# An NSA / RG-LRU decoder layer on one core: x^T split unscaled, the input norm's weight moved into the projection weights, and the residual rebuilt from the two halves

## The chip, the cores and the metric

The kernel runs on one core of one Trainium2 chip. The metric is the device time of one execution in microseconds (us). Single runs of this kernel lie within about 0.3% of each other, so a difference below that can't be told from none.

## What is computed

One step of a one-layer hybrid decoder on a prompt (1024 tokens) and a sample group (8 sequences of 4 tokens), with the same weights. All 1056 tokens go through the same projection; `TOK` is 1056, `D` is 1024. The part that the change touches is the entry of the layer and its first residual:

```python
def rmsnorm(x, g):
    xf = x.astype(jnp.float32)
    y = xf * lax.rsqrt(jnp.mean(xf * xf, axis=-1, keepdims=True) + EPS) * g.astype(jnp.float32)
    return y.astype(x.dtype)
...
u = rmsnorm(x, lw['norm_mix'])
q, q_rot, kv_rows, win_rows, gates, rg, rx = project(u, lw['w_in'], pos)
...
mixed = jnp.concatenate([rmsnorm(o_attn, lw['g_attn']),
                         rmsnorm(jax.nn.gelu(rg) * h_rnn, lw['g_rnn'])], axis=-1)
x = x + mixed @ lw['w_out']
v = rmsnorm(x, lw['norm_mlp'])
x = x + jnp.square(jax.nn.relu(v @ lw['w_up'])) @ lw['w_down']
```

Between them lie three attention branches (compressed, selected, windowed) and a gated linear recurrence (RG-LRU).

## The kernel before

**Precision.** Each float32 product is made of three TensorE products of a value's rounded half and its remainder: `split` (L126) writes `hi` with ScalarE (ACT, L127) and `lo = src - hi` with VectorE (DVE, L128), and `mm3` (L120) adds hi*hi, hi*lo and lo*hi in PSUM.

**Load.** `fetch_x` (L269) reads nine tiles of x, 128 tokens each (the last 32), into eight buffers. `load_x` (L237) takes them in three groups of up to 384 tokens; for each of 8 blocks of 128 features, TensorE transposes (L257) into a PSUM tile `ps_x`. From it ACT writes `u_hi`, scaled by `norm_mix` (`g_mix`, L261), DVE writes `u_lo` (L262), and one of the two copies it unscaled to `xr` (L265), which goes to DRAM as `xT` in twelve DMAs issued by GpSimd (POOL, L267). The row sums of squares come from ACT (L249); the factor 1/rms per token is applied after the projection, through the tile `R`: `bcast_all` (L1150) builds it from diagonal tiles `dg` (DVE, L1159), a product with ones (`ps_bc`, L1160) and an ACT copy (L1162).

**Projection.** `in_proj` (L305) does 128 columns of `w_in` at a time: `w_tile_` (L293) loads the raw tile `wraw` (one buffer, SP queue) and splits it to `wh`, `wl` (two buffers); 72 products follow, in three token chunks of 352, and DVE evacuates each chunk times `R` (L322, L366). There are 18 such tiles: two for the compressed keys and values, four each for the two RG-LRU branches (`rx`, `rg`), two window tiles (`zw`), two more and four for the queries. `gates` (L753) loads 24 columns in the same way.

**Compression of the cached pages.** `cmp_setup` (L449) loads and splits two weight tiles `cwraw` (one buffer; `lo` on POOL); `cmp_cached` (L571) loads 16 tiles of two pages (`lpg`, three buffers; half by the SP queue after a register load for each, L543 and L553, half by POOL, L557), copies them on POOL and DVE (`lpr`, L592), transposes (`ps_ct`, L599) and projects (`ps_c`).

**RG-LRU.** `rglru` (L355) and `rg_gate` (L415) do convolution (DVE, L384), gates, a scan (L405) and products on POOL (L398, L427, L439).

**Residual.** `rnn_proj` (L1164) reads each block of `xT` back (`xres`, L1189), POOL adds the projected RG-LRU result (L1197), and the sum is stored. The small vectors (`vectors`, L190) arrive through nine DMAs of POOL into `rows`, kept in the pool `xrp`.

**Order.** A scheduler places the instructions on each engine's queue, which then runs strictly in that order; `high_priority` lets weight tiles be placed early.

Of the kernel before, what the change touches and what calls it, by code (L numbers as in the profile page):

```python
# [9 lines left out]
F32 = mybir.dt.float32  # L10
# [3 lines left out]
AF = mybir.ActivationFunctionType  # L14
ALU = mybir.AluOpType
# [3 lines left out]
D = 1024  # L19
# [3 lines left out]
TOK = SEQ + NS * QS  # L23
CH = 352
NCH = 3
KT = 8
# [79 lines left out]
class K:  # L106
# [83 lines left out]
    def vectors(self):  # L190
        nc, a = self.nc, self.a
        rows = self.xrp.tile([56, 128], F32, name="rows")
# [44 lines left out]
    def load_x(self):  # L237
        nc, a = self.nc, self.a
        self.u = [self.up.tile([128, KT, TOK], F32R, name=n) for n in ("u_hi", "u_lo")]
        uh, ul = self.u  # L240
        self.stores = {}
        self.xT = self.dp.tile([KT, 128, TOK], F32, name="xT_dram")
        self.ss = self.cp.tile([128, 9], F32, name="ss")
        nc.vector.memset(self.ss, float(D))
        for grp in range(3):
            tiles = self.xt[grp * 3 : grp * 3 + 3]
            for t, (xt, n) in enumerate(tiles):
                junk = self.xtp.tile([128, D], BF16, tag="xj", name="xj", bufs=1)
                nc.scalar.activation(junk[:n], xt[:n], AF.Square, accum_out=self.ss[:n, grp * 3 + t : grp * 3 + t + 1])  # L249
            wdt = sum(n for _, n in tiles)  # L250
            c0 = grp * 384
            for kb in range(KT):
                pool, tag = ((self.ps_tp, "tp"), (self.ps_mm, "mm"))[kb % 2]
                ps = pool.tile([128, 512], F32, tag=tag, name="ps_x")
                o = 0
                for xt, n in tiles:
                    nc.tensor.transpose(ps[:, o : o + n], xt[:n, kb * 128 : kb * 128 + 128], self.ident[:n, :n])  # L257
                    o += n
                g = self.g_mix[:, kb : kb + 1]
                hi, lo = uh[:, kb, c0 : c0 + wdt], ul[:, kb, c0 : c0 + wdt]  # L260
                nc.scalar.activation(hi, ps[:, :wdt], AF.Copy, scale=g)  # L261
                nc.vector.scalar_tensor_tensor(lo, ps[:, :wdt], g, hi.bitcast(F32), ALU.mult, ALU.subtract)  # L262
                if kb % 2 == 0:
                    xr = self.xrp.tile([128, 2, 384], F32, tag="xr", name="xr", bufs=5)
                (nc.scalar.copy if kb % 4 == 0 else nc.vector.tensor_copy)(xr[:, kb % 2, :wdt], ps[:, :wdt])  # L265
                if kb % 2:
                    self.stores[grp, kb] = nc.gpsimd.dma_start(self.xT[kb - 1 : kb + 1, :, c0 : c0 + wdt].rearrange("k p t -> p k t"), xr[:, :, :wdt])  # L267

    def fetch_x(self):  # L269
# [3 lines left out]
        for t in range(9):  # L273
            n = 128 if t < 8 else 32
            xt = self.xtp.tile([128, D], F32, tag="xt", name="xt", bufs=8)
# [17 lines left out]
    def w_tile_(self, c0, m):  # L293
# [5 lines left out]
        nc.sync.dma_start(raw[:, :, :m], src)  # L299
        wh = self.wp.tile([128, KT, 128], F32R, tag="wh", name="wh", bufs=1)  # L300
        wl = self.wp.tile([128, KT, 128], F32R, tag="wl", name="wl", bufs=1)
        self.split(wh[:, :, :m], wl[:, :, :m], raw[:, :, :m])
        return wh, wl

# [144 lines left out]
    def cmp_setup(self):  # L449
# [11 lines left out]
        for i, kv in enumerate("kv"):  # L461
            raw = self.cwp.tile([128, 8, 2, 64], F32, tag="cwraw", name="cwraw", bufs=1)
# [290 lines left out]
    def gates(self):  # L753
# [5 lines left out]
        nc.sync.dma_start(raw[:, :, :24], self.a["w_in"][0].rearrange("(k p) f -> p k f", p=128)[:, :, c0 : c0 + 24])  # L759
        w = self.wp.tile([128, KT, 128], F32R, tag="wh", name="wh", bufs=1)  # L760
# [403 lines left out]
    def rnn_proj(self):  # L1164
# [11 lines left out]
        for dp in range(4):  # L1176
# [8 lines left out]
            for d2 in range(2):  # L1185
# [3 lines left out]
                nc.sync.dma_start(xt, self.xT[d])  # L1189
# [264 lines left out]
    def run(self):  # L1454
# [11 lines left out]
        with ExitStack() as PA:  # L1466
# [3 lines left out]
            with ExitStack() as s:  # L1470
# [5 lines left out]
                with ExitStack() as s2:  # L1476
                    self.xtp = self.pool(s2, "xtp")
                    self.xrp = self.pool(s2, "xrp")
# [6 lines left out]
                    self.vectors()  # L1485
# [5 lines left out]
                zs = [self.z_tile(512 + i * 128, self.zp, "z", 2) for i in range(2)]  # L1491
                self.cmp_cached()
# [136 lines left out]
```

## Time and profile before

| | |
|---|---|
| three runs | 1571.28, 1572.1, 1576.55 us (median 1572.1) |
| profiled execution | 1577.57 us, span 1575.8 us |
| busy share of the span | PE 95%, DVE 57%, ACT 40%, POOL 30% |
| granted TensorE clock, mean | 0.984 |
| DMA | 107.14 MB, 89.79 read and 19.93 written |

PE is TensorE's products, PEld its weight loads. A name like `L592 DVE COPY lpr<-lpg` gives the line of the kernel, the engine, the operation, and what is written from what. SPq is the DMA queue of the SP engine. In a timeline a number in brackets is the idle time of the engine before the instruction, and what ended it.

### The profile page before, as it was taken

The numbers are of one execution on the slowest core, as the hardware profiler recorded it, in microseconds if no ns is written. First come the engines' busy times: TensorE is split into PE (matmuls) and PEld (weight loads), VectorE is DVE, ScalarE is ACT, GpSimd is POOL, SyncE is SP. The second block draws the span as 40 slices with busy tenths as digits, with TensorE's granted clock in tenths as the row PEclk, the third lists the DMA queues.
The fourth block names the chain that finished last, engine by engine and source line by source line (L and its number), as shares of the span: only waits on it lengthen the run. The fifth ranks groups of instructions, "written<-read, shape, count | busy, mean of one in ns | idle before, by whom it ended". The sixth has DMA issues, their size and how long they took to land.

```text
span 1575.8 us, 24404 instructions
## 1 busy us (share of the span) xinstructions
PE 1501.3 (95%) x9439; PEld 1403.2 (89%) x9439; DVE 893.3 (57%) x1674; ACT 623.5 (40%) x1208; POOL 467.0 (30%) x535
## 2 busy tenths in 40 slices
PE   5889999999998999999998999999999999999997
PEld 3879998899766777768898999999999999999997
DVE  7464688657633888899888343433434333343445
ACT  6254685222234888877444031220303122030322
POOL 6450233342624878766673000000000000000012
PEclk9999999999998999999999999999999999999999
DMA  9431111453640000000512020230202021020102
GB/s 294 133 108 37 41 41 30 159 195 103 195 127 1 1 1 1 1 27 27 164 30 79 14 81 27 82 131 14 81 14 81 27 60 49 15 80 14 41 11 101
DMA packets 103768, 107.14 MB, mean 68 GB/s; under 512 B 16112, under 2 KB 90544, under 8 KB 103524
## 3 DMA queue, kind: packets, MB, share of 16 engines
q1 hardware_dynamic: 96718, 89.51, 18.6%
q0 software_dynamic: 4736, 12.86, 2.6%
q10 hardware_dynamic: 2198, 3.20, 0.6%
q8 instruction: 74, 1.21, 0.3%
q14 instruction: 42, 0.34, 0.1%
HBM read 89.79 MB, written 19.93 MB: 70 GB/s over the span
## 4 chain that ended last, share of the span: by engine, by line
PE 77%; DVE 11%; ACT 4%; issue 3%; POOL 2%; DMA 2%; SPq 1%; DVEq 0%; ACTq 0%; POOLq 0%
PE ps_dn L122 8%; PE ps_dn L123 8%; PE ps_dn L124 8%; PE ps_up L122 7%; PE ps_up L123 7%; PE ps_up L124 7%; PE ps_in L122 3%; PE ps_in L123 3%; PE ps_in L124 3%; PE ps_T L1079 3%; PE ps_so L967 2%; PE ps_O L1089 2%; PE ps_S L1047 2%; PE ps_O L1088 1%; PE ps_S L1048 1%
## 5 line engine op out<-in xcount | busy, mean ns | idle before, releaser
L122 PE MATMUL ps_up<-v_hi,wuh 128*128 128x352 f32 x768 | 248.8, 324 | 0.0
L122 PE MATMUL ps_dn<-hh,wdh 128*128 128x352 f32 x768 | 248.3, 324 | 0.0
L123 PE MATMUL ps_up<-v_lo,wuh 128*128 128x352 f32 x768 | 247.0, 322 | 0.0
L124 PE MATMUL ps_up<-v_hi,wul 128*128 128x352 f32 x768 | 246.8, 321 | 0.0
L123 PE MATMUL ps_dn<-hl,wdh 128*128 128x352 f32 x768 | 245.9, 321 | 0.0
L124 PE MATMUL ps_dn<-hh,wdl 128*128 128x352 f32 x768 | 245.5, 321 | 0.0
L1348 DVE TENSOR_TENSOR x<-x,ps_dn 128x352 f32<-128x352 f32 x192 | 99.3, 521 | 222.2 <-PE ps_dn L124 222.1
L1413 POOL TENSOR_TENSOR facc<-facc,fsq 128x352 f32<-128x352 f32 x18 | 17.0, 944 | 700.0 <-ACT fsq L1411 699.8
L127 ACT CAST wdh<-wd 128x1024 fp32r<-128x1024 f32 x32 | 33.5, 1047 | 341.9 <-PE ps_dn L123 288.7
L123 PEld LDWEIGHTS ps_up<-v_lo,wuh 128*128 128x128 f32 x768 | 144.9, 189 | 0.0
L122 PEld LDWEIGHTS ps_up<-v_hi,wuh 128*128 128x128 f32 x768 | 144.6, 188 | 0.0
L124 PEld LDWEIGHTS ps_up<-v_hi,wul 128*128 128x128 f32 x768 | 144.5, 188 | 0.0
L123 PEld LDWEIGHTS ps_dn<-hl,wdh 128*128 128x128 f32 x768 | 144.2, 188 | 0.0
L122 PEld LDWEIGHTS ps_dn<-hh,wdh 128*128 128x128 f32 x768 | 144.1, 188 | 0.0
L124 PEld LDWEIGHTS ps_dn<-hh,wdl 128*128 128x128 f32 x768 | 143.9, 188 | 0.0
L122 PE MATMUL ps_in<-u_hi,wh 128*128 128x352 f32 x432 | 142.8, 331 | 0.9 <-DVE sp_acc L229 0.9
L124 PE MATMUL ps_in<-u_hi,wl 128*128 128x352 f32 x432 | 141.6, 328 | 0.0
L123 PE MATMUL ps_in<-u_lo,wh 128*128 128x352 f32 x432 | 141.4, 327 | 0.0
L128 DVE TENSOR_TENSOR ptl<-ps_T,pth 128x512 fp32r<-128x512 f32 x132 | 88.0, 683 | 13.7 <-ACT pth L127 12.6
L127 ACT CAST pth<-ps_T 128x512 fp32r<-128x512 f32 (+1 forms) x148 | 83.3, 588 | 18.7 <-PE ps_T L1079 14.8
L122 PEld LDWEIGHTS ps_in<-u_hi,wh 128*128 128x128 f32 x432 | 83.2, 193 | 1.5 <-issue 1.3
L123 PEld LDWEIGHTS ps_in<-u_lo,wh 128*128 128x128 f32 x432 | 83.3, 193 | 0.1
(506 smaller groups left out, 3320.6 us busy)
## 6 DMA issues: line engine op xcount, KB each, us to landing
wu<-in_w_up_dram SPq DMA_DIRECT2D x32, 512.0 KB
wd<-in_w_down_dram SPq DMA_DIRECT2D x32, 512.0 KB
wraw<-in_w_in_dram SPq DMA_DIRECT2D x18, 512.0 KB
lpg<-in_cache_kv_dram SPq DMA_DIRECT2D x64, 128.0 KB
xres<-xT_dram SPq DMA_DIRECT2D x8, 528.0 KB
x_dram<-xres SPq DMA_DIRECT2D x8, 528.0 KB
x<-x_dram SPq DMA_DIRECT2D x3, 1408.0 KB
xt<-in_x_prompt_dram SPq DMA_DIRECT2D x8, 512.0 KB
```

The source lines that it names most:

```text
L122: t.matmul(out, wh, xh, start=first, stop=False)
L123: t.matmul(out, wh, xl, start=False, stop=False)
L124: t.matmul(out, wl, xh, start=False, stop=last)
L127: self.nc.scalar.copy(hi, src)
L128: (eng or self.nc.vector).tensor_tensor(lo, src, hi.bitcast(F32), ALU.subtract)
L967: T.matmul(po[w, :128], l, r, start=n == 0, stop=n == len(ops) - 1, tile_position=(0, s4 * 32))
L1047: T.matmul(pv, qr[:, h], kh[:, ks], start=True, stop=False)
L1048: T.matmul(pv, qr[:, h], kl[:, ks], start=False, stop=not (far or dia))
L1079: T.transpose(ps[:K, h * 128 : h * 128 + 128], src(h), self.ident)
L1089: T.matmul(O, v, pl, start=False, stop=last)
L1348: V.tensor_tensor(x1[:, d, sl], x1[:, d, sl], ps[:, :CH], ALU.add)
L1413: P.tensor_tensor(acc, acc, sq, ALU.add)
```

## The change

Five edits. (1) `u_hi` and `u_lo` are a plain split of the transposed x; no `g_mix`, no copy to `xr`, no `xT` in DRAM. (2) `scale_w` multiplies each raw weight tile by `g_mix`, in place, on POOL, before its split. (3) The residual `xres` is `u_hi + u_lo`, by one DVE addition of 128x1056 for each of eight blocks, in place of a DMA. (4) `xt` gets nine buffers and `cwraw` two. (5) `vectors` is called after the first two projections, with `rows` in another pool.

```diff
@@ vectors
-        rows = self.xrp.tile([56, 128], F32, name="rows")
+        rows = self.ccp.tile([56, 128], F32, name="rows")
@@ load_x
-                g = self.g_mix[:, kb : kb + 1]
-                hi, lo = uh[:, kb, c0 : c0 + wdt], ul[:, kb, c0 : c0 + wdt]
-                nc.scalar.activation(hi, ps[:, :wdt], AF.Copy, scale=g)
-                nc.vector.scalar_tensor_tensor(lo, ps[:, :wdt], g, hi.bitcast(F32), ALU.mult, ALU.subtract)
-                if kb % 2 == 0:
-                    xr = self.xrp.tile([128, 2, 384], F32, tag="xr", name="xr", bufs=5)
-                (nc.scalar.copy if kb % 4 == 0 else nc.vector.tensor_copy)(xr[:, kb % 2, :wdt], ps[:, :wdt])
-                if kb % 2:
-                    self.stores[grp, kb] = nc.gpsimd.dma_start(self.xT[kb - 1 : kb + 1, :, c0 : c0 + wdt].rearrange("k p t -> p k t"), xr[:, :, :wdt])
+                self.split(uh[:, kb, c0 : c0 + wdt], ul[:, kb, c0 : c0 + wdt], ps[:, :wdt])
@@ fetch_x
-            xt = self.xtp.tile([128, D], F32, tag="xt", name="xt", bufs=8)
+            xt = self.xtp.tile([128, D], F32, tag="xt", name="xt", bufs=9)
@@ w_tile_
         nc.sync.dma_start(raw[:, :, :m], src)
+        self.scale_w(raw[:, :, :m])
...
+    def scale_w(self, raw):
+
+        self.nc.gpsimd.tensor_tensor(raw, raw, self.g_mix.unsqueeze(2).to_broadcast(list(raw.shape)), ALU.mult)
@@ cmp_setup
-            raw = self.cwp.tile([128, 8, 2, 64], F32, tag="cwraw", name="cwraw", bufs=1)
+            raw = self.cwp.tile([128, 8, 2, 64], F32, tag="cwraw", name="cwraw", bufs=2)
@@ gates
+        self.scale_w(raw[:, :, :24])
@@ rnn_proj
-                nc.sync.dma_start(xt, self.xT[d])
+                V.tensor_tensor(xt, self.u[0][:, d].bitcast(F32), self.u[1][:, d].bitcast(F32), ALU.add)
@@ run
                     self.cmp_setup()
-                    self.vectors()
...
                 zs = [self.z_tile(512 + i * 128, self.zp, "z", 2) for i in range(2)]
+                self.vectors()
                 self.cmp_cached()
```

The edits also move other instructions, since the scheduler orders every queue anew. In the changed program a line number is up to five lower than before (L592 is L587, L1159 is L1155, L543 is L538).

The SP queue at the start of the program, before (`wraw` is a raw weight tile, `xt` the tiles of x, `pt` the page table, `cwraw` the two compression weights, `lpg` the cached pages):

```order
L299 DMA wraw<-in_w_in_dram 128x8x128
L276 DMA xt<-in_x_prompt_dram 128x1024 x8
L299 DMA wraw<-in_w_in_dram 128x8x128
L519 DMA pt<-in_page_table_dram 1x64
L466 DMA cwraw<-in_w_ck_dram 64x8x64 x4
L276 DMA xt<-in_x_sample_dram 32x1024
```

and with the change:

```order
L289 DMA wraw<-in_w_in_dram 128x8x128
L266 DMA xt<-in_x_prompt_dram 128x1024 x8
L266 DMA xt<-in_x_sample_dram 32x1024
L514 DMA pt<-in_page_table_dram 1x64
L461 DMA cwraw<-in_w_ck_dram 64x8x64 x4
L461 DMA cwraw<-in_w_cv_dram 64x8x64 x4
```

The second compression weight (`in_w_cv`), which stood 43 rows further down, behind the first six page loads and fourteen register loads, now comes ahead of all page loads. The second `wraw` moved from ahead of `pt` to behind the first four page loads, and the loads of the fourth, fifth and sixth page tile, which stood behind sixteen more register loads, now come in pairs between them.

The DVE queue during the first projection, before (`dg` are the diagonal tiles from which `R` is made, `lpr1` the copies of the fourth, fifth and sixth page tile, `z` the evacuation of the first chunk):

```order
L592 COPY lpr1_793<-lpg_791 128x256
L1159 TENSOR_SCALAR dg_481<-ident_60,rxy_460 128x128
L1159 TENSOR_SCALAR dg_484<-ident_60,rxy_460 128x128
L592 COPY lpr1_906<-lpg_904 128x256
L592 COPY lpr1_942<-lpg_940 128x256
L1159 TENSOR_SCALAR dg_489<-ident_60,rxy_460 128x128
L1159 TENSOR_SCALAR dg_492<-ident_60,rxy_460 128x128
L322 TENSOR_TENSOR z_507<-ps_in_514,R_473 128x352
```

and with the change:

```order
L1155 TENSOR_SCALAR dg_387<-ident_60,rxy_366 128x128
L1155 TENSOR_SCALAR dg_390<-ident_60,rxy_366 128x128
L128 TENSOR_TENSOR wl_504<-wraw_500,wh_503 128x1024
L587 COPY lpr1_855<-lpg_853 128x256
L1155 TENSOR_SCALAR dg_395<-ident_60,rxy_366 128x128
L1155 TENSOR_SCALAR dg_398<-ident_60,rxy_366 128x128
L317 TENSOR_TENSOR z_413<-ps_in_421,R_379 128x352
L587 COPY lpr1_891<-lpg_889 128x256
```

The copy of the sixth page tile moved from ahead of the first evacuation to behind it; that of the fourth stands a few rows ahead of this piece.

The POOL queue within RG-LRU, with the change (the products `t` and `X` are L398 and L427 of before; before, the same rows stand there without the `wraw` ones):

```order
L357 COPY X<-stT 128x8x3
L298 TENSOR_TENSOR wraw<-wraw,g_mix 128x1024 x2
L396 MEMSET A 128x8x3
L422 TENSOR_TENSOR X<-X,t_1993 128x1024
L424 TENSOR_TENSOR X<-X,t_1993 128x32
L393 TENSOR_TENSOR t_2171<-t_2171,t_2170 128x1080
L397 MEMSET t_2171 128x8x2
L398 COPY t_2171<-stT 128x8
```

Seven of the eighteen full scalings and the short one of the gates stand between the first convolution and the last product of RG-LRU. Of the others one stands in the load, one behind the split of the second compression weight, three among the page copies, and six in the part from `rnn_proj` to the queries. The nine DMAs of `vectors` stay where they were on POOL, directly behind those of `cmp_setup`.

## Rows read from the trace of the kernel before

**Rows 1.** The page: busy us of each engine, share of the span, instructions.

```profile
PE 1501.3 (95%) x9439; PEld 1403.2 (89%) x9439; DVE 893.3 (57%) x1674; ACT 623.5 (40%) x1208; POOL 467.0 (30%) x535
```

**Rows 2.** Windows: stretch, length, busy us of PE, PEld, DVE, ACT, POOL, clock, DMA share, GB/s.

```profile
0.00:20.00 20.00, 10.70 (x43) 7.90 (x43) 9.48 (x25) 14.66 (x27) 9.87 (x21) 1.00 0.97 313
20.00:40.00 20.00, 11.87 (x42) 7.13 (x43) 19.81 (x64) 12.72 (x28) 16.40 (x22) 1.00 0.94 276
```

**Rows 3.** Timeline of the load: start, duration, engine, line, operation.

```profile
7.16 1.06 ACT L249 ACTIVATE xj<-xt 128x1024 bf16<-128x1024 f32 x1 [0.78 <-DMA xt<-in_x_prompt_dram]
...
31.14 2.38 POOL L128 TENSOR_TENSOR cwkl<-cwraw,cwkh 128x1024 fp32r<-128x1024 f32 x1
31.31 2.58 DVE L592 COPY lpr<-lpg 128x256 f32<-128x256 f32 x1
...
38.92 0.45 DVE L265 COPY xr<-ps_x 128x288 f32<-128x288 f32 x1
...
39.51 0.63 PE L122 MATMUL ps_in<-u_hi,wh 128*128 128x352 f32 x1 [0.89 <-DVE sp_acc L229]
```

**Rows 4.** Groups of DVE and ACT in 0 to 39.6 us: count, busy us, mean ns.

```profile
L265 DVE COPY xr<-ps_x 128x384 f32<-128x384 f32 x12 | 6.6, 547 | 0.0
...
L265 DVE COPY xr<-ps_x 128x288 f32<-128x288 f32 x4 | 1.8, 442 | 0.0
...
L265 ACT COPY xr<-ps_x 128x384 f32<-128x384 f32 x4 | 2.0, 511 | 0.0
...
L265 ACT COPY xr<-ps_x 128x288 f32<-128x288 f32 x2 | 0.8, 396 | 0.0
```

**Rows 5.** The chain in order of time, 33 to 64 us: start, us, what.

```profile
33.79 0.66 SPq L466
...
48.19 4.95 DMA lpg<-in_cache_kv_dram
53.23 0.58 DVE lpr L592
...
61.64 1.04 ACT wh L127
62.68 0.49 ACT R L1162
```

**Rows 6.** Windows, as rows 2, within the first projections and the compression.

```profile
53.00:60.00 7.00, 5.70 (x21) 5.74 (x22) 4.31 (x11) 0.00 (x0) 4.25 (x9) 0.53 0.13 40
...
80.00:112.00 32.00, 29.72 (x231) 27.29 (x229) 20.88 (x48) 16.81 (x40) 19.87 (x35) 0.95 0.42 124
```

**Rows 7.** Waits of PE, 40 to 60 us: in total, times, longest.

```profile
PE ps_bc L1160 <- DVE dg L1159: 3.2, 1, 3.2
```

**Rows 8.** RG-LRU: window as rows 2; group of L384; its durations min/median/max.

```profile
160.00:275.00 115.00, 109.11 (x666) 107.33 (x665) 90.20 (x119) 77.40 (x114) 40.03 (x42) 0.99 0.12 32
...
L384 DVE SCALAR_TENSOR_TENSOR xc<-X,vec,xc 128x360 f32<-128x360 f32 x30 | 28.3, 942 | 6.8 <-ACT xc L382 6.5
...
L384 DVE SCALAR_TENSOR_TENSOR xc<-X,vec,xc x36: 576/593/2967, 152.1 to 253.9; 128x360 f32<-128x360 f32 x36
```

**Rows 9.** Timeline of POOL and DVE around 234 us.

```profile
234.17 2.53 POOL L398 TENSOR_TENSOR t<-t,t 128x1080 f32<-128x1080 f32 x1
...
234.22 0.53 DVE L322 TENSOR_TENSOR X<-ps_in,R 128x352 f32<-128x352 f32 x1 [2.49 <-PE ps_in L124]
234.66 2.43 DVE L384 SCALAR_TENSOR_TENSOR xc<-X,vec,xc 128x360 f32<-128x360 f32 x1
```

**Rows 10.** Groups of POOL in 0 to 300 us.

```profile
L267 POOL DMA_DIRECT2D xT_dram<-xr x12 | 8.9, 745 | 9.0 <-ACT xr L265 5.6 <-DVE xr L265 2.4 <-DVE rxt L141 0.5
...
L128 POOL TENSOR_TENSOR cwvl<-cwraw,cwvh 128x1024 fp32r<-128x1024 f32 x1 | 2.4, 2392 | 2.2 <-ACT cwvh L127 2.2
```

**Rows 11.** Who waited for `xres`, and the window of `rnn_proj` as rows 2.

```profile
POOL xres L1197: 7.7, 4
...
300.00:350.00 50.00, 49.66 (x314) 49.42 (x313) 22.83 (x35) 9.45 (x11) 23.27 (x25) 1.00 0.61 203
```

More of the change, by code (lines that the diff above doesn't have):

```diff
@@ L240, in load_x @@
         uh, ul = self.u
-        self.stores = {}
-        self.xT = self.dp.tile([KT, 128, TOK], F32, name="xT_dram")
         self.ss = self.cp.tile([128, 9], F32, name="ss")
@@ L1477, in run @@
                     self.xtp = self.pool(s2, "xtp")
-                    self.xrp = self.pool(s2, "xrp")
                     self.cwp = self.pool(s2, "cwp")
```

## The prediction

> **What bounds the kernel now.** I read the page's busy shares first, then busy time by stretch, then the timeline, the chain, the waits and the groups in the stretches that the change touches. TensorE (PE) is busy 95% of the span [rows 1]; the change touches the first 400 us, and there three places matter. In the load (0 to 39.5 us) no projection runs yet: the DMA engines are 97% and 94% busy, and in the second half DVE works 19.81 of 20 us [rows 2]; the first projection starts at 39.51, right behind a DVE copy to `xr` that ended at 39.37 [rows 3]. In the first projections PE stands still for 3.2 us, waiting for the diagonal tiles `dg` [rows 7]; the chain shows why: DVE's queue stands at a copy of a page whose DMA was issued late by the SP queue, with the second compression weight in its way [rows 5]. After that pause the granted clock is 0.53 over 7 us [rows 6], the lower of its two levels (1.2 and not 2.4 GHz) for nearly all of it. RG-LRU (160 to 275 us) is PE-bound, but with DVE busy 90.2 of 115 us [rows 8].
>
> **The change, part by part.** The sum is made against the profiled execution, 1577.57 us, which is 5.5 us over the median of the three runs, 1572.1; I carry the difference over to the median. About 0.3%, 4.7 us, is what a measurement of this kernel can tell from no change.
>
> *A. Start of the first projection: -4 us (0 to -7.5).* DVE loses sixteen `xr` copies ahead of 39.5 us, 6.6 + 1.8 = 8.4 us [rows 4]. The split's subtraction costs about what the scaled one did: no gain counted. DVE was full, so at most 8.4 us could go. ACT loses six copies, 2.0 + 0.8 us [rows 4], out of 14.66 + 12.72 us of work [rows 2], and gains the early cast of the second compression weight, about 1 us: 25.6 us. It can start on x at 7.16 us [rows 3] and has done at most 1 or 2 us of this before; so it ends at 31 to 33 us, and the last subtraction at 32 at the earliest: that is the end of the range, -7.5. Between the last subtractions DVE has copies of the third page tile. Its loads stand behind the second compression weight and the second `wraw` on the SP queue, and POOL now puts two 2.4 us operations on end, the split of that weight and a scaling [rows 10]; while one runs, such a copy waits (2.58 us beside POOL's 2.38 [rows 3]). I place the third tile's copy at 34 to 35 us, and the first projection at 35.5. The other end, 0, is a page that comes so late that 39.5 stays. The twelve DMA issues taken from POOL, 8.9 us [rows 10], pay for the first scalings there (at 2.39 us each [rows 10], the nearest operation: the same 128x1024, two operands); the first one runs while x is still arriving.
>
> *B. The pause behind the first projection: -7.5 us (0 to -9).* Removed: the wait of 3.2 us [rows 7]; the slow clock after it, 7 us at 0.53, in which full clock would have needed 0.53 * 7 = 3.7, so 3.3, of which I count 2.8, since the start of the first projection can stay slow; and a wait behind ACT's cast of the third weight tile, which stood ahead of the copy to `R` (1.04 and 0.49 us [rows 5]), 1.5 us, since that copy now precedes the cast. The cause goes away: the second compression weight no longer waits for its only buffer at 33.79 us [rows 5], and the page loads behind it come up to 9 us sooner, against a projection that starts 4 us sooner; the sixth page's copy stands behind the first evacuation. What is late next is the fifth page, about 44 us, just before PE would need `R` (about 45). If it comes 4 us later, B is gone; hence 0.
>
> *C. Compression: +1 us (0 to +7).* Three scalings, 7.2 us of POOL, stand among the page copies. POOL works 19.87 of 32 us there [rows 6], so they have room, but a page tile freed late is loaded late: a little is put on the path.
>
> *D. RG-LRU: +3 us (0 to +17).* Seven scalings and a short one. POOL's two-operand work holds up DVE: a 128x360 operation that takes 0.593 us in the median [rows 8] took 2.43 beside POOL's 2.53, while one that reads PSUM took its 0.53 under the same POOL operation [rows 9]. By how much on average: thirty of L384 took 28.3 us in place of 30 * 0.593 = 17.8 [rows 8], with some ten POOL products in the stretch (the code has L398 and L427 four times, L439 three times), so about 1.1 us a product. Seven scalings: 7.7 us more for a DVE that has 115 - 90.2 = 24.8 us free [rows 8]. I put 3 us on PE, for stretches where an evacuation or a weight split is late. The worst, all 7 * 2.39 = 16.7 us on the path, is the end of the range. A gain is excluded, as nothing is removed there.
>
> The Trainium skill ("SBUF — State Buffer", section "SBUF: two separate sides") calls the pair of ports that VectorE and GpSimd share an exclusive lock, taken for a whole instruction, which a VectorE operation with two SBUF inputs or in a two-port mode needs. The trace agrees [rows 9]. By that rule alone, each scaling could cost DVE its full 2.4 us, which is the second rival below.
>
> *E. Residual: 0 (0 to +2).* Eight additions of 1056 columns, by L384's 0.593 us for 360 columns [rows 8] some 1.7 us each, fit a DVE that works 22.83 of 50 us, beside a PE that works 49.66 of them [rows 11]. The DMA reads that go were waited for by POOL, 7.7 us [rows 11], and POOL held up nobody there; so 4.3 MB less to read is worth nothing, and the writes count in A and B alone. If the additions came late, stores would be late, which nobody awaits until 100 us later.
>
> *F. The six other scalings: +0.5 us (0 to +3).* A raw tile lies ready well before its cast, which waits for PE. The small vectors' DMAs do not move; costed at nothing, they hide behind the rows of x.
>
> Sum: -4 - 7.5 + 1 + 3 + 0 + 0.5 = -7.0 us: 1570.6 for the profiled execution, and 1572.1 - 7.0 = **1565.1 us** against the median.
>
> The Trainium skill ("GPSIMD Engine Reference", section "Engine selection") speaks against edit 2: elementwise work on two operands belongs on VectorE, which is about twice as fast. The trace shows 2.39 us on POOL [rows 10]; no run here shows the scaling itself on either engine.
>
> **The rivals.**
>
> *One: the pages set the pace.* PE starts sooner, but the cached pages, half issued by a SP queue of register loads and half by POOL between scalings, arrive as before, and PE waits later what it gained. For it: the chain ran from 33.79 to 53 us through SP [rows 5], and POOL has more on its queue. Against it: DMA had room after the load, and the second compression weight is out of the way. A and B give back 8 of their 11.5 us: 1573 us, no change.
>
> *Two, slower: the lock in RG-LRU.* If DVE meets each of the seven scalings (16.7 us), or POOL stands at a scaling whose tile has not landed, with the products of the scan behind it, DVE or POOL becomes the bound there. It decides when the added DVE time passes the 24.8 us free, or when it falls on the stretches where evacuations are due. With +16.7 for D: -11.5 + 1 + 16.7 + 0.5 = +6.7, 1579 us. For it: DVE is at 78% and some operations were already four times as long. Against it: only 1.1 us per product so far.
>
> *Three: a larger gain.* A at -6, B at -9, D at 0 and C at 1: -13.5, 1559 us.
>
> That the change does not do what it says applies to the small vectors alone: their DMAs stay in place, and I count nothing for them.
>
> **How the numbers follow.** Forecast 0.57 (0.53 of it faster by over 0.3%, 0.04 within), rival one 0.21, two 0.13, three 0.09. Faster: 0.53 + 0.09 = 0.62; within 0.3%: 0.04 + 0.21 = 0.25; slower: 0.13. The range reaches from beyond rival three (1556) to just short of rival two (1577), which holds A and B together down to 0 with C and D as priced (+4.5).
>
> **What would show it.** A: the first product of the first projection near 35.5 us. B: no wait of PE for `dg` over 1 us, and no stretch at 0.5 clock directly after it; the second weight tile's products some 11 us earlier than now. C and D: PE waits in 80 to 125 us as before; L384's mean in RG-LRU from 942 to some 1100 ns with PE busy still over 93%. E: `rnn_proj` as full as before. I am wrong if the first projection starts at 38 or later, if PE stands still for pages, or if RG-LRU grows by over 6 us.

## The result, and the profile after

The change is slower: median 1597.48 us of four runs (1591.43 to 1601.6), beside 1573.35 us for the kernel before in four runs; the ratio is 1.0139 (95% interval 1.0108 to 1.0170). The prediction was 1565.1 us, 1556 to 1577. The profiled execution took 1596.68 us with a span of 1594.8, 19.0 us over the span of before; its mean clock is 0.975 (0.984 before).

Engines on the page of the changed kernel, answering to [rows 1]:

```profile
PE 1503.9 (94%) x9439; PEld 1403.6 (88%) x9439; DVE 915.5 (57%) x1664; ACT 619.7 (39%) x1202; POOL 496.9 (31%) x542
```

TensorE's busy time is 2.6 us more than before; the other 16 us are waits. Where they lie is read from the first and last starts of its products (us; from the views of the tiles `ps_in`, `ps_g`, `ps_k`):

| stretch | before | after | difference |
|---|---|---|---|
| start to first projection | 39.5 | 40.4 | +0.9 |
| first projection to RG-LRU's first `ps_g` | 119.7 | 118.7 | -1.0 |
| RG-LRU, first to last `ps_g` | 97.1 | 106.2 | +9.1 |
| last `ps_g` to first page of the sample attention (`ps_k`) | 156.9 | 165.0 | +8.1 |
| first `ps_k` to the end of the span | 1162.6 | 1164.5 | +1.9 |

The third and the fourth stretch are to be read together: `ps_g` marks the recurrence alone, and while it is late PE goes on with products of later tiles. Windows from the first to the last `ps_g` (columns as [rows 2]), before and with the change:

```profile
159.20:256.30 97.10, 92.66 (x563) 91.16 (x562) 76.42 (x107) 68.78 (x103) 31.46 (x33) 0.98 0.13 35
```

```profile
159.10:265.30 106.20, 97.36 (x589) 95.05 (x588) 88.64 (x110) 69.80 (x103) 47.37 (x40) 0.98 0.12 31
```

Of the 9.1 us, PE spends 4.7 on 26 more products, which the next stretch then lacks, and it stands 4.4 us longer. From the first `ps_g` to the first `ps_k` it is 254.0 us before and 271.2 with the change, +17.2.

**The load.** Windows of the changed kernel (columns as [rows 2]) and, in its timeline, DVE, POOL and PE around the wait that took the gain:

```profile
20.00:40.00 20.00, 6.52 (x32) 3.88 (x32) 17.64 (x43) 9.18 (x20) 16.58 (x18) 0.68 0.59 150
```

```profile
28.33 2.35 POOL L128 TENSOR_TENSOR cwkl<-cwraw,cwkh 128x1024 fp32r<-128x1024 f32 x1
...
31.84 2.33 POOL L128 TENSOR_TENSOR cwvl<-cwraw,cwvh 128x1024 fp32r<-128x1024 f32 x1
34.14 1.89 POOL L298 TENSOR_TENSOR wraw<-wraw,g_mix 128x1024 f32<-128x1024 f32 x1
...
28.34 2.95 DVE L587 COPY lpr<-lpg 128x256 f32<-128x256 f32 x2
31.20 4.85 DVE L273 TENSOR_SCALAR ms<-ss 128x9 f32<-128x9 f32 x1
...
37.48 0.42 DVE L128 TENSOR_TENSOR u_lo<-ps_x,u_hi 128x288 fp32r<-128x288 f32 x1
...
37.96 1.79 PE L255 MATMUL ps_x<-ident,xt 128*128 128x128 f32 x6 [9.22 <-DVE u_lo L128]
```

The copies are gone and DVE has less to do, yet it stands: an operation of 128x9, `ms`, "takes" 4.85 us, as long as POOL's `cwvl` and the second scaling run one behind the other. The last parts of `u_lo`, for which the transposes wait, stand behind it in DVE's queue. Before, `cwkl` and `cwvl` began 11.7 us apart (31.14 and 42.81).

**The raw tile.** Loads of `wraw` by the SP queue, with the cast of the first raw tile; before:

```profile
0.74 0.45 SPq L299 DMA_DIRECT2D wraw<-in_w_in_dram  x1
8.48 0.38 SPq L299 DMA_DIRECT2D wraw<-in_w_in_dram  x1
...
25.41 0.53 SPq L299 DMA_DIRECT2D wraw<-in_w_in_dram  x1
...
5.34 1.04 ACT L127 CAST wh<-wraw 128x1024 fp32r<-128x1024 f32 x1 [1.93 <-DMA wraw<-in_w_in_dram]
```

and with the change, with the product that waits for the third load:

```profile
27.13 0.54 SPq L289 DMA_DIRECT2D wraw<-in_w_in_dram  x1
...
47.65 0.42 SPq L289 DMA_DIRECT2D wraw<-in_w_in_dram  x1
...
10.61 1.92 POOL L298 TENSOR_TENSOR wraw<-wraw,g_mix 128x1024 f32<-128x1024 f32 x1
...
21.15 1.11 ACT L127 CAST wh<-wraw 128x1024 fp32r<-128x1024 f32 x1
...
52.34 1.90 POOL L298 TENSOR_TENSOR wraw<-wraw,g_mix 128x1024 f32<-128x1024 f32 x1 [6.01 <-DMA wraw<-in_w_in_dram]
54.18 1.84 POOL L587 COPY lpr<-lpg 128x256 f32<-128x256 f32 x5
```

`wraw` has one buffer. Before, the first tile was cast at 5.34 us, while ACT waited for x; now the product comes first, at 10.61, and the cast finds its place among x's at 21.15. So the second and third raw tiles are loaded 19 and 22 us later, and POOL stands 6.01 us at the third product, with page copies behind it.

**The compression.** The timeline around 82 us, where PE waited longest:

```profile
80.17 1.90 POOL L298 TENSOR_TENSOR wraw<-wraw,g_mix 128x1024 f32<-128x1024 f32 x1 [1.13 <-DMA wraw<-in_w_in_dram]
80.66 1.59 DVE L587 COPY lpr<-lpg 128x256 f32<-128x256 f32 x1 [2.14 <-DMA lpg<-in_cache_kv_dram]
...
82.17 0.60 DVE L495 SCALAR_TENSOR_TENSOR cq<-cq,cx 64x256 f32<-64x256 f32 x1
...
82.81 0.42 ACT L496 ACTIVATE cq<-cq 64x256 f32<-64x256 f32 x1 [3.56 <-DVE cq L495]
83.25 0.59 ACT L503 CAST xj0h<-ps_ct 128x512 fp32r<-128x512 f32 x1
...
83.89 0.39 PE L122 MATMUL ps_c<-xj0h,cwkh 128*128 128x256 f32 x1 [3.52 <-ACT xj0h L503]
```

A page comes late, DVE waits for it, a product on POOL holds up its copy until 82.1, ACT waits for DVE, and PE for a cast that stands behind ACT's wait. The clock falls behind the gap, to 0.88 and 0.78 in these windows; the same windows of before, below, have 0.91 and 0.87:

```profile
80.00:100.00 20.00, 13.97 (x94) 11.92 (x93) 12.40 (x27) 9.23 (x21) 12.33 (x20) 0.88 0.30 87
100.00:120.00 20.00, 17.64 (x110) 14.61 (x109) 10.89 (x24) 9.40 (x22) 5.99 (x12) 0.78 0.16 54
```

```profile
80.00:100.00 20.00, 18.95 (x147) 17.99 (x146) 12.80 (x30) 9.73 (x24) 11.34 (x21) 0.91 0.46 132
100.00:120.00 20.00, 16.79 (x116) 13.75 (x114) 12.82 (x28) 11.61 (x27) 8.63 (x16) 0.87 0.21 66
```

In these 40 us PE does 204 products, 263 before: most of its lead of 6.5 us at the first product of the compression (`ps_c`, 71.3 in place of 77.8) goes there.

**RG-LRU.** Window 160 to 285 us of the changed kernel as [rows 8], and groups of DVE in it:

```profile
160.00:285.00 125.00, 114.64 (x696) 111.84 (x695) 101.70 (x121) 78.88 (x115) 56.12 (x50) 0.99 0.12 32
```

```profile
L379 DVE SCALAR_TENSOR_TENSOR xc<-X,vec,xc 128x360 f32<-128x360 f32 x30 | 26.2, 872 | 9.3 <-ACT xc L377 8.9
L389 DVE SCALAR_TENSOR_TENSOR t<-t,xc 128x360 f32<-128x360 f32 x12 | 12.4, 1036 | 2.3 <-ACT t L386 2.2
...
L391 DVE SCALAR_TENSOR_TENSOR t<-xc,t 128x360 f32<-128x360 f32 x12 | 9.7, 811 | 0.5 <-ACT xc L390 0.3
...
L128 DVE TENSOR_TENSOR xl<-xc,xh 128x360 fp32r<-128x360 f32 x11 | 8.7, 792 | 1.8 <-ACT xh L127 1.7
```

The same groups of the kernel before, 160 to 275 us:

```profile
L394 DVE SCALAR_TENSOR_TENSOR t<-t,xc 128x360 f32<-128x360 f32 x12 | 6.4, 531 | 4.1 <-ACT t L391 4.1
L396 DVE SCALAR_TENSOR_TENSOR t<-xc,t 128x360 f32<-128x360 f32 x12 | 6.3, 527 | 1.5 <-ACT xc L395 1.3
...
L128 DVE TENSOR_TENSOR xl<-xc,xh 128x360 fp32r<-128x360 f32 x11 | 5.8, 525 | 1.4 <-ACT xh L127 1.1
```

The hold-ups fell on other operations than the prediction watched: the convolution (L379) even fell from 942 to 872 ns (2.1 us in all), while these three groups grew by 12.3 us.

**The residual.** DVE after RG-LRU, in the timeline of the changed kernel:

```profile
290.18 2.42 DVE L1185 TENSOR_TENSOR xres<-u_hi,u_lo 128x1056 f32<-128x1056 f32 x2
...
292.52 1.31 DVE L661 STREAM_SHUFFLE rt<-zw 128x1056 f32<-128x1056 f32 x1
293.74 0.49 DVE L771 TENSOR_TENSOR gt<-ps_gt,gt 24x352 f32<-24x352 f32 x1
```

Two of the additions stand ahead of the gates `gt`, for which PE waits (2.6 us in all at `ps_out`, by its waits).

### The profile page after: what moved, and what is told of

It is laid out like the page before. It is cut to its first block, busy times and chain, and to the rows that moved or that the text cites. A ratio compares the mean times of both kernels' runs of the same rounds, so it can differ in the third digit from the quotient of the medians.

```text
span 1594.8 us, 24341 instructions
## 1 busy us (share of the span) xinstructions
PE 1503.9 (94%) x9439; PEld 1403.6 (88%) x9439; DVE 915.5 (57%) x1664; ACT 619.7 (39%) x1202; POOL 496.9 (31%) x542
## 4 chain that ended last, share of the span: by engine, by line
PE 71%; DVE 15%; ACT 4%; DMA 4%; issue 3%; POOL 2%; SPq 1%; DVEq 0%; ACTq 0%; POOLq 0%
PE ps_dn L122 8%; PE ps_dn L123 8%; PE ps_dn L124 8%; PE ps_up L122 7%; PE ps_up L123 7%; PE ps_up L124 7%; PE ps_T L1075 3%; PE ps_in L122 2%; PE ps_in L123 2%; PE ps_in L124 2%; PE ps_so L963 2%; PE ps_O L1085 2%; PE ps_S L1043 2%; PE ps_O L1084 1%; PE ps_S L1044 1%
## 5 line engine op out<-in xcount | busy, mean ns | idle before, releaser
L124 PE MATMUL ps_dn<-hh,wdl 128*128 128x352 f32 x768 | 245.6, 321 | 0.0
```

Source lines behind the costliest of these rows:

```text
L124: t.matmul(out, wl, xh, start=False, stop=last)
```

## The experiments

Four groups of four, each group on one chip. On the chips of the second and third the kernel before itself takes 1593.78 and 1593.61 us (1575.7 and 1576.41 on the others), so the ratios to it, taken on the same chip, are compared; the profile `before_again` is for these. Single runs spread by more than the 0.3% named at the start (before, on the first group's chip: 1571.24 to 1586.81 us), so the intervals decide. The stages are from one profile each; the kernel before itself starts RG-LRU at 159.2 us on one chip and 156.0 on another, so some 3 us in that column tell nothing across chips. The two last columns are to be read together, as above. Starts and lengths are in us.

| run | ratio to before (95%) | first projection | first `ps_g` | RG-LRU | last `ps_g` to first `ps_k` |
|---|---|---|---|---|---|
| change | 1.0139 (1.0108 to 1.0170) | 40.4 | 159.1 | 106.2 | 165.0 |
| no_scale | 0.9999 (0.9976 to 1.0023) | 30.1 | 147.6 | 98.0 | 160.7 |
| scale_dve | 1.0111 (1.0078 to 1.0143) | 39.8 | 149.4 | 108.6 | 164.5 |
| xres_act | 1.0082 (1.0057 to 1.0107) | 40.3 | 159.5 | 106.4 | 158.9 |
| scale_ts | 1.0215 (1.0182 to 1.0248) | 37.8 | 160.1 | 102.7 | 176.3 |
| before_mul | 1.0143 (1.0118 to 1.0168) | 46.2 | 164.8 | 105.1 | 164.6 |
| u_scaled | 1.0030 (1.0007 to 1.0052) | 40.5 | 153.9 | 97.0 | 164.8 |
| u_late | 1.0001 (0.9983 to 1.0019) | 39.1 | 156.0 | 96.9 | 159.0 |
| u_late_cwdve | 0.9978 (0.9961 to 0.9995) | 41.1 | 150.1 | 95.5 | 157.5 |
| before_again | (the kernel before) | 39.8 | 156.0 | 97.1 | 156.9 |
| x_first | 1.0127 (1.0095 to 1.0158) | 31.2 | 161.2 | 106.5 | 166.3 |
| scale_act | 1.0103 (1.0074 to 1.0132) | 41.4 | 159.5 | 110.8 | 159.2 |
| best_x | 0.9934 (0.9911 to 0.9957) | 35.1 | 145.7 | 97.1 | 159.0 |
| scale_front | 1.0059 (1.0037 to 1.0081) | 40.3 | 157.6 | 98.6 | 161.8 |
| scale_rg | 1.0053 (1.0029 to 1.0078) | 31.4 | 147.2 | 107.0 | 160.4 |
| raw2_front | 1.0120 (1.0092 to 1.0149) | 42.0 | 150.6 | 106.2 | 167.6 |
| best_y | 0.9938 (0.9917 to 0.9958) | 35.1 | 144.4 | 95.4 | 159.0 |

### First group: which edit, and which engine

**no_scale.**

```diff
-        self.nc.gpsimd.tensor_tensor(raw, raw, ...)
+        pass
```

> The changed kernel with the eighteen products of the weights with norm_mix (and the short one of the gates) left out: norm_mix is then not applied at all. Theory (GpSimd's product holds up VectorE): the wait of 9.2 us before the last transposes of x shrinks to 5 or less, RG-LRU's t*xc (1036 ns) and xc*t (811 ns) come back to 530 ns, RG-LRU is 5 to 6 us shorter, in all 12 to 16 us less: 1582 to 1586. Rival one (the eight additions hi + lo in VectorE's queue are the loss): at most 5 us less, 1592 or more. Rival two (the order of the page loads is the loss): first projection at 39 us or later as now, time 1593 or more.

1577.6 us, ratio 0.9999: the products cost the whole 1.4%, more than the 12 to 16 us expected, and the rest of the change nets to nothing. RG-LRU is back at 98.0, and so are the three groups of DVE that had grown; from 147.6 to 245.6 us:

```profile
L389 DVE SCALAR_TENSOR_TENSOR t<-t,xc 128x360 f32<-128x360 f32 x11 | 5.8, 527 | 4.3 <-ACT t L386 4.3
L391 DVE SCALAR_TENSOR_TENSOR t<-xc,t 128x360 f32<-128x360 f32 x11 | 5.8, 529 | 1.1 <-ACT xc L390 0.9
L128 DVE TENSOR_TENSOR xl<-xc,xh 128x360 fp32r<-128x360 f32 x11 | 5.8, 528 | 1.8 <-ACT xh L127 1.7
```

The first projection comes at 30.1, though DVE is held up here too. In its timeline:

```profile
29.55 0.46 DVE L128 TENSOR_TENSOR u_lo<-ps_x,u_hi 128x288 fp32r<-128x288 f32 x1 [0.24 <-ACT u_hi L127]
29.92 5.28 DVE L143 SCALAR_TENSOR_TENSOR rxy<-rxt,rxy 128x9 f32<-128x9 f32 x1
```

All parts of `u_lo` but one stand ahead of the 5.28 us in which `cwkl` and `cwvl` hold DVE; in the change four stood behind. The order in the queue decides what a hold-up costs.

**scale_dve.**

```diff
-        self.nc.gpsimd.tensor_tensor(raw, raw, ...)
+        self.nc.vector.tensor_tensor(raw, raw, ...)
```

> The changed kernel with the products of the weights done by VectorE (one 128x1024 product, about 1.2 us by the weight split's 1.22) in place of GpSimd. Theory (GpSimd holds up VectorE): VectorE does 18 * 1.2 = 22 us more itself, but in RG-LRU 7 * 1.2 = 8.4 us in place of the 10 us by which its own operations were stretched; first projection near 37 us, time 1584 to 1590. Rival one (the additions): no change, 1595 to 1599. If VectorE is the bound in RG-LRU, whoever does the product, it is as slow as the change, 1595 or more, with RG-LRU as long as now.

1594.29 us, ratio 1.0111, slower than expected. One product takes 1225 ns in the median on DVE, 1899 on POOL, but RG-LRU is as long as with POOL's (108.6): the seven products lengthen it whether DVE does them or is held up by them. The Trainium skill ("GPSIMD Engine Reference", section "Engine selection") would have this work on VectorE, as about twice as fast. Here POOL takes 1.55 times as long, so the direction agrees, but the time of the kernel hardly gains by it.

**xres_act.**

```diff
-                V.tensor_tensor(xt, u_hi[:, d], u_lo[:, d], ALU.add)
+                S.copy(xt, u_hi[:, d])
```

> The changed kernel with the residual taken as hi alone, copied by ScalarE (the lo part of x is left out of the residual), so that VectorE has no additions. Theory (the products are the larger loss, the two additions ahead of the gates a smaller one): the gates' tanh chain is 2.4 us earlier, ps_ms to the end of the output product 2 to 5 us shorter, time 1592 to 1595. Rival one (the additions are the loss): 10 us or more less, 1587 or less. If the additions are hidden: 1597.

1588.95 us, ratio 1.0082: a larger gain than expected, between the two theories. Last `ps_g` to first `ps_k` takes 158.9 in place of 165.0, so the additions cost 6.1 us there; the ratios say 9 in all, with intervals that allow 6.

**scale_ts.**

```diff
-        self.nc.gpsimd.tensor_tensor(raw, raw, ...)
+        for k in range(KT): self.nc.gpsimd.tensor_scalar_mul(raw[:, k], raw[:, k], self.g_mix[:, k : k + 1])
```

> The changed kernel with each product on GpSimd cut into eight 128x128 products with one scalar per partition (one operand from SBUF per instruction, 8 * about 0.3 us). Theory: if VectorE is held up for the length of one instruction of GpSimd with two operands, these short ones hold it up for 0.3 us at most; RG-LRU's t*xc returns to about 550 ns, time 1584 to 1590. If any work of GpSimd on SBUF holds up VectorE for its whole length, or if the order is what costs: 1595 to 1600.

1610.75 us, ratio 1.0215. A piece takes 602 ns in the median, twice what was assumed, eight of them 4.8 us in place of 1.9. RG-LRU is a little shorter (102.7) and DVE is held less, though not as little as expected: from 160 to 285 us `t*xc` takes 884 ns (1036 in the change) and `xc*t` 550 (811). But POOL is slower by more: ACT's casts wait 40.3 us for the products, 11.9 in the change. What the hold-up alone costs it doesn't tell.

### Second group: the products alone, and the change without them

**before_mul.** In the kernel before, behind each load of a raw tile:

```diff
+        self.nc.gpsimd.tensor_tensor(raw, raw, ones8, ALU.mult)
```

> The kernel before, with eighteen products of 128x1024 on GpSimd added between each raw weight tile and its split, by a vector of ones, and nothing else of the change. Theory (the products are the loss and the rest of the change nets to about nothing): 1588 to 1596, with RG-LRU (first to last product of ps_g) some 105 us in place of 97. Rival (the products hurt only together with the other edits: the second compression weight beside them, the additions): 1573 to 1580, RG-LRU 97 to 100.

Ratio 1.0143: the products alone, in the kernel before, cost what the change costs. RG-LRU 105.1 beside 97.1 in before_again.

**u_scaled.**

```diff
-        self.scale_w: raw *= g_mix
+        load_x: hi = g * ps; lo = g * ps - hi
+        rnn_proj: xres = hi + lo (DVE); xres *= 1 / g (ACT)
```

> The change with its second edit turned back: norm_mix multiplied into hi and lo as x is copied, as in the kernel before; no product of weights; the residual is (hi + lo) / norm_mix, by an addition on VectorE and a scaling by 1/norm_mix on ScalarE; no x^T in DRAM. Theory: as the run without products: 1573 to 1579, first projection at 30 to 32 us, and the lead lost where the pages of the sample attention come in (415 to 435 us). If the load's gain came from the missing scaling of x and not from the products: first projection at 36 or later and 1580 or more.

Ratio 1.0030, RG-LRU 97.0. The first projection came at 40.5 on this chip, not at 30 to 32: ahead of five parts of `u_lo` in DVE's queue a page copy waited 2.23 us for its page, and then this copy and `ms` took 4.95 us beside POOL's `cwkl` and `cwvl`. So a late start needs no products of weights: in this order of DVE's queue, the page and the split of the compression weights are enough.

**u_late.**

```diff
-                V.tensor_tensor(xt, hi, lo, ALU.add); S.activation(xt, xt, AF.Copy, scale=1/g)
+                S.activation(xt, hi, AF.Copy, scale=1/g)
...
+                    V.scalar_tensor_tensor(t, lo[sl], 1/g, t, ALU.mult, ALU.add)
```

> As the run before it, with the residual put together behind the gates: ScalarE copies hi / norm_mix, and VectorE adds lo / norm_mix to each product tile of 128x352 after the evacuation, so that no 128x1056 addition stands ahead of the gates. If what is gained ahead of 413 us reaches the end: 3 to 8 us less than the run before it, 1565 to 1571. If the pages of the sample attention set the pace from 413 us on: the first transposed page comes 3 to 6 us earlier and the time stays within 2 us of it, 1572 to 1578.

Ratio 1.0001, and 159.0 in place of 164.8 from the last `ps_g` to the first `ps_k`: the additions' price again (5.8, here together with ACT's scaling behind them). By the medians, 3.3 us of it reached the end (0.3%, with intervals that overlap).

**u_late_cwdve.** The `lo` of `cwraw` by DVE.

```diff
-            self.split(wh, wl, rv, nc.gpsimd)
+            self.split(wh, wl, rv)
```

> As the run before it, with the lo parts of the two compression weights made by VectorE (two subtractions of 128x1024 at about 1.2 us) in place of GpSimd (two at 2.4). Theory (GpSimd's two-operand work in the load holds up VectorE): first projection 2 to 4 us earlier than in the run before it, the time the same if the pages absorb it, 2 to 4 us less if not.

Ratio 0.9978. The hold-up in the load is gone (`ms` takes 0.37 us), but the first projection is not earlier (41.1): two parts of `u_lo` now stand behind a page copy that waits 3.96 us for its page. In its profile, the fastest of its ten runs, six us were gained further on, up to RG-LRU; the medians differ by 4.0.

### Third group: the order, and ScalarE

> The kernel before, unchanged, for a profile of it beside the three others of this group. Where pages from DRAM set the pace its stages may be longer than in the profile shown first; first projection at 38 to 41 us, RG-LRU (first to last product of ps_g) 96 to 98 us.

As expected. Beside the first profile, it is the sample attention that makes these chips slower: first to last `ps_k` takes 74.2 us, 58.9 in the first.

**x_first.**

```diff
+                    last_lo = ... u_lo ...
-                self.norm_x()
+                with tc.issue_after(last_lo): self.norm_x()
... (vectors() and the page copies on DVE alike)
```

> The changed kernel with VectorE's queue in the load put in another order by hand: the page copies, the rsqrt chain and the small vectors stand behind the last lo part of x; every product of weights is kept. Theory (the load lost not by work but because the last lo parts stood behind copies that GpSimd's products held up): first projection at 30 to 33 us in place of 40.4, the lead then 7 to 10 us up to RG-LRU, time 8 to 10 us under the change, ratio to before 1.007 to 1.009. Rival (the lo parts themselves are held up, wherever they stand): first projection at 36 or later.

The first projection comes at 31.2, nine us earlier, with every product kept: the order was what the load lost by. But the ratio is 1.0127, no gain clear of the noise. PE's waits, 8 to 150 us:

```profile
PE ps_bc L1156 <- DVE dg L1155: 5.7, 2, 3.0
...
PE ps_c L122 <- ACT xj1h L503: 4.2, 2, 3.3
PE ps_in L122 <- DVE z L317: 3.7, 1, 3.7
```

What was put behind `u_lo` is awaited next, and RG-LRU starts at 161.2. Nine us at the first projection gained nothing at RG-LRU's start. scale_dve shows the reverse: first projection at 39.8, and RG-LRU starts at 149.4.

**scale_act.**

```diff
-        self.scale_w(raw); self.split(wh, wl, raw)
+        for k in range(KT):
+            nc.scalar.activation(wh[:, k], raw[:, k], AF.Copy, scale=g[:, k])
+            nc.vector.scalar_tensor_tensor(wl[:, k], raw[:, k], g[:, k], wh[:, k], ALU.mult, ALU.subtract)
```

> The changed kernel with norm_mix multiplied in while the weights are split: ScalarE writes hi with a scale, 8 instructions of 128x128, VectorE writes lo from raw and norm_mix, 8 instructions of 128x128; GpSimd has no products. Theory (a product that holds up nobody's queue costs little): RG-LRU 98 to 102 us, ratio to before 1.003 to 1.008. If the split is late because ScalarE's eight pieces take over 2.5 us where the cast took 1.04: RG-LRU 104 or more, ratio 1.012 or more.

Ratio 1.0103, and RG-LRU 110.8, longer than with POOL: the theory as put there fell. The second case came in RG-LRU, though the ratio stayed under its 1.012. Groups of ACT and DVE, 159 to 270 us:

```profile
L294 ACT ACTIVATE wh<-wraw,g_mix 128x128 fp32r<-128x128 f32 x56 | 17.1, 390 | 0.5 <-PE ps_in L123 0.5
...
L295 DVE SCALAR_TENSOR_TENSOR wl<-wraw,g_mix,wh 128x128 fp32r<-128x128 f32 x56 | 17.5, 379 | 0.0
```

Eight pieces take 3.1 us on ACT, where the cast took 1.04, and 3.0 on DVE, where the subtraction took 1.45 on average. Which of the two delays RG-LRU is not separated. PE loses little within it, though: it does 70 more products there than before (633 and 563) and stands 5.6 us. The loss comes behind it, in one wait for the gates (its window as [rows 8], and from PE's waits up to the first `ps_k`):

```profile
159.50:270.30 110.80, 105.20 (x633) 103.74 (x632) 93.09 (x165) 82.64 (x156) 30.35 (x35) 0.97 0.12 30
...
PE ps_out L122 <- DVE gt L773: 8.2, 1, 8.2
```

From the first `ps_g` to the first `ps_k` it is 270.0 us, 273.1 in scale_dve and 271.2 in the change (258.7 in no_scale): on none of the engines tried was this work free. On POOL only the gates' short product was left.

**best_x.** u_late_cwdve with the order of x_first.

> No products of weights (norm_mix in hi and lo, the residual as hi / norm_mix by ScalarE and lo / norm_mix added on VectorE behind the gates), the lo parts of the compression weights by VectorE, and VectorE's queue in the load ordered by hand as in the run x_first. Theory: first projection at 29 to 32 us, every stage up to 413 us earlier than in the kernel before, ratio to before 0.990 to 0.995. If the pages of the sample attention set the pace from 413 us on: ratio 0.997 to 1.000, with the stage from the first to the last ps_k longer by the lead.

Ratio 0.9934: faster than both kernels. The first projection comes at 35.1, later than expected.

### Fourth group: how the loss divides

**scale_front** and **scale_rg.**

```diff
-        self.scale_w(raw[:, :, :m])
+        if self.nw <= 5: self.scale_w(raw[:, :, :m])         # scale_front
+        if self.nw in range(6, 13): self.scale_w(raw[:, :, :m])  # scale_rg
```

> The changed kernel with norm_mix multiplied into the first five weight tiles alone (load and compression); it is left out of the thirteen full tiles behind them (the gates' short product stays). Theory (the change's 1.4% is made of a lead of some 11 us that the first five products use up, 8 to 9 us in RG-LRU, and the rest behind it): RG-LRU (first to last product of ps_g) back at 96 to 99 us, its start no earlier than in the kernel before; ratio to before 1.004 to 1.008. If the products ahead of RG-LRU cost nothing: ratio 1.000 to 1.002, RG-LRU starting 9 us or more earlier than in the kernel before.

> The changed kernel with norm_mix multiplied into weight tiles six to twelve alone (those of RG-LRU and the two behind it in the same stretch; the gates' short product stays); it is left out of the other eleven full tiles. Theory: RG-LRU starts 8 to 12 us earlier than in the kernel before and lasts 104 to 107 us; ratio to before 1.003 to 1.007. The excess of this run and of scale_front over the run without products should add up to 9 to 14 thousandths. If the products hurt RG-LRU only together with the late pages: RG-LRU 97 to 99, ratio 1.000 to 1.002.

Both as expected: 1.0059 and 1.0053. Over no_scale these are 6.0 and 5.4 thousandths, 11.4 in all of the change's 14.0; the rest, some 4 us, is left for the six products behind RG-LRU, and lies within the intervals (which leave about 8 us either way). The first five products use up ten us of lead (first `ps_g` at 157.6, not 147.2), the next seven make RG-LRU longer by 9 (107.0 in place of 98.0, with 22 more products in it) and the whole kernel by some 8.5.

**raw2_front.**

```diff
-        raw = self.wrp.tile(..., tag="wraw", bufs=1)
+        raw = (self.ccp if self.nw == 2 else self.wrp).tile(..., tag="wraw", bufs=1)
```

> The changed kernel with a raw tile of its own for the second weight tile, so that its load and the third tile's do not wait for the product and the split of the first (one of six buffers for page copies is given up for the space); all products are kept. Theory (the single raw tile, held until the product of the first tile has norm_mix, makes the raw loads late by some 20 us, and GpSimd stands at the third product for 6 us with the pages behind it): that wait of GpSimd goes, RG-LRU starts 3 to 6 us earlier than in the change, ratio to before 1.009 to 1.012. Rival (only VectorE's hold-ups and its own work count): no change, 1.013 to 1.015.

RG-LRU starts at 150.6, 8.5 us earlier than in the change, although the first projection is later (42.0) and all products are kept. Its raw loads, and the windows that fell in the change:

```profile
0.74 1.09 SPq L290 DMA_DIRECT2D wraw<-in_w_in_dram  x2
...
25.42 0.53 SPq L290 DMA_DIRECT2D wraw<-in_w_in_dram  x1
```

```profile
80.00:100.00 20.00, 17.42 (x136) 15.09 (x136) 16.42 (x37) 12.24 (x29) 15.90 (x24) 1.00 0.53 146
100.00:120.00 20.00, 18.72 (x149) 16.18 (x148) 10.88 (x24) 10.75 (x27) 2.21 (x8) 1.00 0.02 8
```

So with a second raw tile most of the loss ahead of RG-LRU is gone. The scheduler also placed the products anew, so how much is the wait and how much the new order is not separated. scale_dve, with one raw tile, points the same way: its first product begins at 7.93 and the first cast at 10.30, the next two raw tiles are loaded at 14.98 and 36.78 (27.13 and 47.65 in the change), and RG-LRU starts at 149.4; so one tile costs little where the product and the cast come early (there POOL has no products either). At the end less is left: the ratio 1.0120 is 3 us under the change's, with an interval that overlaps it.

**best_y.** As best_x, but `norm_x` and `vectors` where the scheduler puts them.

> As best_x, with the page copies alone ordered behind the last lo part of x; the rsqrt chain and the small vectors keep the scheduler's places. Theory (in best_x the first evacuation waited 7.1 us for the broadcast of the rsqrt, which stood behind the page copies): that wait under 4 us, RG-LRU starting 2 to 4 us earlier, ratio to before 0.990 to 0.993. If the compression waits for pages anyway: as best_x, 0.993 to 0.995.

1566.36 us, ratio 0.9938. The wait for `dg` fell from 7.1 to 1.7 us, RG-LRU starts 1.3 us earlier, and the ratio is that of best_x. Both versions divide by `norm_mix` in the residual, so they need weights without a zero.

## Why the prediction was wrong

The step that failed is the price of the eighteen products. In A the first ones were paid for by the DMA issues taken from POOL, and C, D and F gave the others 4.5 us together; with them and without them (no_scale) the kernel differs by 1.4%, some 22 us. E, priced at 0, is about 6. What A and B were to give was there: without the products RG-LRU starts at 147.6 us, 11.6 ahead of before (-11.5 forecast), though of this lead 7.0 us are left at the first `ps_k` and 0.2 at the end of the span.

**A, the start of the first projection (-4): +0.9.** That removing the copies frees DVE was right, and was undersized: without products the first projection comes at 30.1, beyond the bound of -7.5. What failed is the price of the hold-up. The step saw POOL's two operations on end, `cwvl` and the second scaling, but charged them with the wait of one page copy, placed at 34 to 35 us. DVE was held until 36.05, and four parts of `u_lo` with their transposes, 4.4 us more, stood behind that. The sign of error that the prediction named, a first projection at 38 or later, came. x_first shows that the order alone is nine us, and that nine us at this place do not reach RG-LRU.

**B, the pause behind the first projection (-7.5): there, then lost.** No wait for `dg` over 1 us is left, and from the first product of the first weight tile to that of the second it is 17.4 us in place of 25.0. By RG-LRU's start nothing of it remains.

**C, the compression (+1, 0 to +7): about +6,** what is left when B is taken from the stretch, by one profile each. POOL had room, as priced; but a queue runs in order, and the price of a product is its wait for the raw tile (6.01 and 1.13 us), with the copies behind it, and what it holds up on DVE. The missed step is that a product between load and split keeps the only raw tile: the first cast came at 21.15 us in place of 5.34. The order of the SP queue had shown the second `wraw` move, and the prediction gave it no price. In raw2_front, with its new order, RG-LRU starts 8.5 us earlier.

**D, RG-LRU (+3, 0 to +17): some 8.5** by scale_rg, uncertain by about 5. The mechanism was right (the three groups of DVE are back at 527 to 529 ns without the products), the size off threefold: these groups grew by 12.3 us, less 2.1 in the convolution, as against 7.7 estimated, and the recurrence by 9.1. The 1.1 us a product had been read from the convolution, whose mean is 838 ns without the products (no_scale) and 872 with them, so it doesn't measure them. PE covered about half of that with products taken ahead and lacked them behind. "24.8 us free" on DVE is a sum over the stretch; that it had none where evacuations and splits are due is argued, not shown: RG-LRU is as long with no full product on POOL (scale_dve +11.5 over before, scale_act +13.7). "RG-LRU grows by over 6 us" was a sign of error too.

**E, the residual (0, 0 to +2): about +6** (xres_act 6.1, u_late 5.8). The additions were costed by how full DVE is in `rnn_proj`; two of them are ahead of it, in front of the gates, where they take 2.42 us of DVE and PE waits 2.6 at `ps_out`. Where the rest of the 6 arises is open.

**F, the other six scalings (+0.5, 0 to +3): some 4,** by the difference of ratios, uncertain by about 8; "a raw tile lies ready well before its cast" held no longer.

Of the rivals, two (the hold-up in RG-LRU, 0.13) named the right sign and one of the two large terms, at 16.7 us in place of some 8.5; the other, the first five products (6.0 thousandths in scale_front), it did not see. One (pages set the pace) is not borne out ahead of RG-LRU: no_scale starts it 11.6 us earlier with the same pages to read, and best_x leads before_again by 8.2 us at the first `ps_k` (401.8 and 410.0) and by 12.7 at the end of the span. In no_scale's profile the sample attention took 64.8 us, 6 more than before, and ate most of its lead; why is open. By the Trainium skill ("SBUF — State Buffer", section "SBUF: two separate sides") the lock is held for a whole instruction and the loser stands. The 4.85 us of `ms` during two POOL instructions agree; what stood behind `ms`, and so waited too, the rule does not tell.

## What to carry to other kernels

Work moved onto a side engine is priced by what it stands in front of: the single buffer that it keeps, the queue behind it, and the busier engine's order around it; its own busy time does not tell it. Ask of each new step between a load and its first use whether the buffer now lives longer, and when the step can start: here the weights could be cast at 5.34 us, the product began at 7.9 on DVE (scale_dve) and at 10.61 on POOL, behind its DMA issues. An engine that is 80% busy over a stretch may still have no time where its result is due; adding the suspected work alone to the old kernel, as in before_mul, shows what it costs. And a stretch that ends with the last product of one chain measures that chain: count the products in it before calling its growth a loss.

## What was not expected of the hardware

- Eight products of 128x128 with a scalar per partition on POOL take 602 ns each in the median, together 2.5 times the one product of 128x1024 with two operands (1899 ns).
- Chips differ: the kernel before took 1593.8 and 1593.6 us on two of them and 1575.7 and 1576.4 on two others; in the profiles the sample attention, which reads pages, is 74.2 us on one and 58.9 in the first.
